# The first norm's gain and bias onto the residual: VectorE in sixteen pieces in place of GpSimd in eight

## The chip, the cores and the metric

One core of one Trainium2 chip runs the whole kernel. The metric is the device time of one execution in microseconds, as the median of several runs; the profile is of one further execution. Lower is better. The engines are called TensorE (PE in the rows, PEld for its weight loads), VectorE (DVE), ScalarE (ACT), GpSimd (POOL) and SyncE (SP, here only a queue that issues DMAs).

## What is computed

One decoder layer over 512 tokens of width 2048, all in float32. Cut to what matters here:

```python
mix = concat(sgu, hgrn2, mla) @ w_out
x   = layer_norm(ALPHA * x + mix, ln1_g, ln1_b)          # first norm
# mixture of experts: 32 experts, every token goes to 2 of them
for each expert e, on its own rows xb of x:
    h = silu(xb @ w_gate[e]) * (xb @ w_up[e])             # 2048 -> 512
    out[rows] += gate * (h @ w_down[e])                   # 512 -> 2048
x   = layer_norm(ALPHA * x + out, ln2_g, ln2_b)           # second norm
```

## The kernel before

**Where the first norm's vectors go.** The normalised rows without gain and bias are written to a DRAM tensor `x1d`, from which the experts gather their rows; gain and bias are put onto those by columns (`gcol`, in `rows`). The same normalised rows stay in SBUF as `z`, four tiles of 128 x 2048, one for each 128 tokens, since the second norm adds the experts' output to them. These copies must get gain and bias too, at any time before the last stage. Lines 1551 to 1559 do this in the expert loop: after expert 12's gate and up products the two vectors `ln1_g` and `ln1_b` are broadcast by DMA from the SP queue to two tiles of 128 x 2048 (`gb1`, 1 MB each), and in experts 13 to 20 GpSimd multiplies and adds one half (128 x 1024) of one `z` tile in each. After expert 21's products the same two slots are loaded with `ln2_g` and `ln2_b`, which the last stage reads (`lng2, lnb2`).

**One expert.** The loop over `e` calls `up(e)` (gate and up products, 16 weight chunks of 128 x 1024) and then `down(e - 1)` (8 chunks). A chunk is 512 KB. `Ring.pump` (lines 66 to 103) moves them: it issues the load from the SP queue as soon as a raw buffer is free (L81), and as soon as one of four pairs is free it splits the chunk into a high part (ScalarE copy, L96) and a low part (VectorE subtraction, L97), after which the raw buffer is free again. Four of the eight down chunks stay whole and are multiplied in full float32 (L1426). So an expert has 20 splits. A pair comes free when TensorE is done with the chunk (`ring.done`), so the splits run up to four pairs ahead of TensorE, and every instruction stands in its engine's queue in the order in which this program calls it.

**What else VectorE does in an expert.** `L1374` once at the start of `up(e)`; `L1364` half of the next expert's transposed rows; `L162` the low parts of those rows and of the hidden layer; `L1407` the product of gate and up for the next `down` (`turn_h`, called inside `down`, at its third chunk). ScalarE has the matching `L161`, and `L1430`, which takes each of the four 512-column outputs of `down` out of PSUM.

**What else GpSimd does.** In each expert a memset (L1328) and a gather (L1323) for expert e + 2 ahead of `up(e)`, and two scatter-adds (L1338) in `down(e - 1)`, which wait for L1430. The two multiplications and additions of lines 1558 and 1559 stand between them.

**Order around the change.** The lines stand after `up(e)` and after its pending `L162`, and ahead of `down(e - 1)`. On GpSimd the instruction in front of them is the gather, which is done early in the expert; on VectorE the one in front would be the last `L162` of `up(e)`, and the next ones the first two splits that `down(e - 1)` sets free.

Of the kernel before, what the change touches and what calls it, by code (L numbers as in the profile page):

```python
# [14 lines left out]
OP = mybir.AluOpType  # L15
# [8 lines left out]
DM = 2048  # L24
# [105 lines left out]
def build(tc, I, out):  # L130
    with ExitStack() as ctx:
        _build(tc, tc.nc, ctx, I, out)


def _build(tc, nc, ctx, I, out):
# [8 lines left out]
    def slot(tag, shape, dt=F32):  # L144
        cnt[0] += 1
        return bp.tile([P] + list(shape), dt, tag=tag, name=f"{tag}_{cnt[0]}")
# [5 lines left out]
    tt, ts, stt = nc.vector.tensor_tensor, nc.vector.tensor_scalar, nc.vector.scalar_tensor_tensor  # L152
# [74 lines left out]
    for k2 in range(8):  # L227
        t = slot(f"X{k2}", [2, 2, 512], F32R)
# [48 lines left out]
    def bcast(ap, n):  # L277
        return bass.AP(tensor=ap.tensor, offset=ap.offset, ap=[[0, P], [1, n]])
# [674 lines left out]
    z = [slot(t, [DM]) for t in ("B5", "B6", "B8", "B9")]  # L953
# [10 lines left out]
    gb1 = [slot("X7", [DM]), slot("B2", [DM])]  # L964
# [317 lines left out]
    def gates():  # L1282
        nc.gpsimd.tensor_tensor(gv, oh, wide(gate, [2 * NB, NE], 2), op=OP.mult)
        hl = tp[:, 0:512].rearrange("p (i a e) -> p i a e", a=2, e=NE)
        yield
        act(hl[:, :, 0], gv, AF.Copy)
        nc.gpsimd.tensor_tensor(hl[:, :, 1], gv, hl[:, :, 0].bitcast(F32), op=OP.subtract)
        yield
        o = aux()
        for i in range(2 * NB):  # L1290
            mm(o[:, 0:2 * NE], ohr[:, i // NB, i % NB], hl[:, i].rearrange("p a e -> p (a e)"),
               start=i == 0, stop=i == 2 * NB - 1)
        nc.vector.tensor_copy(gt, o[:, 0:NE])
        tt(gt, gt, o[:, NE:2 * NE], op=OP.add)
        yield
# [25 lines left out]
    def gather(e):  # L1321
        def move(n):
            nc.gpsimd.indirect_dma_start(out=xgs[e % 2][0:n, :], out_offset=None, in_=x1d[:],  # L1323
                                         in_offset=off(idx[0:n, EX[e]:EX[e] + 1]),
                                         bounds_check=T - 1, oob_is_err=False)
        if e:
            if e > 1:
                nc.gpsimd.memset(xgs[e % 2], 0.0)  # L1328
            sized(e, move)
        else:  # L1330

            move(32)
            with tc.If(nc.gpsimd.value_load(cnt_i[0:1, EX[0]:EX[0] + 1]) > 32):
                move(P)
# [20 lines left out]
    def rows(e, i, *by):  # L1355

        n = 4 // len(by)
        tmp = xgs[e % 2][:, i * 512:(i + 1) * 512]
        for h, ts in enumerate(by):
            o = turn(xgs[e % 2], i, range(h * n, h * n + n))  # L1360
            for j in range(h * n, h * n + n):
                g, b = [gcol[:, a, 4 * i + j:4 * i + j + 1] for a in range(2)]
                s = slice(j * P, (j + 1) * P)
                ts(tmp[:, s], o[:, s], g, b, op0=OP.mult, op1=OP.add)  # L1364
        def parts():
            d = [xT[i // 2][:, 4 * (i % 2):4 * (i % 2) + 4, :, a] for a in range(2)]
            split(d[0], d[1], tmp.rearrange("p (a t) -> p a t", t=P))
        return parts

    def up(e, hooks):  # L1370


        n = nc.tensor.value_load(cnt_i[0:1, EX[e]:EX[e] + 1])
        stt(folds[e % 2], pairs, few[:, EX[e]:EX[e] + 1], ident, op0=OP.mult, op1=OP.add)  # L1374
        for which in range(2):
            o = acc()
            for c in range(8):
                if (which, c) in hooks:
                    hooks[which, c]()
                if (which, c) == (1, 2):  # L1380
                    act(raws[0], fold(e, 0), AF.Silu)
                w = ring.get()
                ks = [(2 * c + j, [v[:, j * 512:(j + 1) * 512] for v in w]) for j in range(2)]
                with tc.If(n > HALF) as more:
                    for k, wk in ks:
                        mm3(o, [xT[k // 8][:, k % 8, :, a] for a in range(2)], wk, k == 0, k == KD - 1)
                with more.Else():
                    for k, wk in ks:
                        x = xT[k // 8][:, k % 8, 0:HALF].rearrange("p t a -> p (t a)")
                        mm(o, x, wk[0], start=k == 0, stop=False)  # L1390
                        mm(o, x, wk[1], start=False, stop=k == KD - 1)  # L1391
                if c == 7:
                    act(raws[which], o, AF.Copy)
                ring.done()
# [10 lines left out]
    def turn_h(e):  # L1405
        hi, lo = [v.rearrange("p a t -> p (a t)") for v in hTs[e % 2]]
        tt(hfs[e % 2], raws[0], fold(e, 1), op=OP.mult)  # L1407
        split(hi, lo, hfs[e % 2])
# [3 lines left out]
    def down(e):  # L1412
        if e in (0, NE - 1):
            yts.append(slot("M0" if e else "M1", [DM]))
        for n in range(4):
            o = acc()
            hT = hTs[e % 2]
            for c in range(2):
                if (n, c) == (1, 0) and e + 1 < NE:
                    turn_h(e + 1)  # L1420
                w = ring.get()
                for j in range(2):
                    k = 2 * c + j
                    cs = slice(j * 512, (j + 1) * 512)
                    if n in WHOLE:
                        mm(o, hfs[e % 2][:, k * P:(k + 1) * P], w[:, cs], start=k == 0, stop=k == 3)  # L1426
                    else:
                        mm3(o, (hT[0][:, k, :], hT[1][:, k, :]), (w[0][:, cs], w[1][:, cs]), k == 0, k == 3)
                if c:
                    act(yts[-1][:, n * 512:(n + 1) * 512], o, AF.Copy, scale=gt[:, EX[e]:EX[e] + 1])  # L1430
                ring.done()
            if e == NE - 1 and n == 1:
                scatter(e, 0)
        scatter(e, *([1] if e == NE - 1 else [0, 1]))
# [4 lines left out]
    def steps_of(e):  # L1439

        steps = {}
        for i in range(4):
            steps[(0, 2 * i + 1) if e > 1 else [(0, 5), (0, 6), (0, 7), (1, 1)][i]] = lambda i=i: later.append(rows(e, i, ts, gain_act))
            steps[1, 2 * i + 2] = lambda: later.pop(0)()
        return steps
# [74 lines left out]
    for e in range(NE):  # L1520
        if e and e + 2 < NE:
            gather(e + 2)
        hooks = steps_of(e + 1) if e + 1 < NE else {}
        if e == 0:
            rows(0, 1, gain_act)()
            hooks[0, 0] = lambda: later.append(rows(0, 2, ts, gain_act))

            def part3():
                later.pop()()
                later.append(rows(0, 3, ts, gain_act))  # L1530
            hooks[0, 2] = part3

            def last():
                later.pop()()
                gather(2)
            hooks[0, 4] = last
            gate_table = gates()
            for c in (0, 5, 7):
                hooks[1, c] = lambda: next(gate_table)
        if e == 1:  # L1540
            hooks[0, 2] = lambda: turn_h(0)
        up(e, hooks)
        while later:
            later.pop(0)()
        if e == 9:
            for entry in lent:
                entry[1] = True
        if e == NE - 3:
            for entry in ers:
                entry[1] = True  # L1550
        if e in (12, 21):
            gb1 = [slot("X7", [DM]), slot("B2", [DM])]
            for t, name in zip(gb1, ("ln1_g", "ln1_b") if e == 12 else ("ln2_g", "ln2_b")):
                nc.sync.dma_start(t, bcast(I[name], DM))
        if 13 <= e < 21:
            s = [slice(0, DM // 2), slice(DM // 2, DM)][(e - 13) % 2]
            b = (e - 13) // 2
            nc.gpsimd.tensor_tensor(z[b][:, s], z[b][:, s], gb1[0][:, s], op=OP.mult)  # L1558
            nc.gpsimd.tensor_tensor(z[b][:, s], z[b][:, s], gb1[1][:, s], op=OP.add)
        if e == 0:  # L1560
            x4 = slot("X4", [2, 1024])
            ring.add([x4[:, 0, :]])
            hfs += [x4[:, 1, i * DE:(i + 1) * DE] for i in range(2)]
            ring.add([misc[:, 1024:]])
            ring.pump()
        elif e < NE - 1:
            down(e - 1)
# [201 lines left out]
```

## Time and profile before

| | us |
|---|---|
| median of 3 runs | 1982.48 |
| lowest, highest | 1977.16, 1982.84 |
| the profiled execution | 1979.87 |
| its span, first to last instruction | 1978.1 |

The experts take some 1100 us of the span; in the experts VectorE is busy for some 86% and TensorE for some 96% of the time, and the granted TensorE clock is full except in short stretches. A row of the windows view gives, for a stretch in us from the span's start, the busy time of each engine with its count of instructions, the granted clock, the mean busy share of the DMA engines (its records overlap, so that it can pass 1) and GB/s. A row of the timeline gives start, duration, engine, line, operation, output and inputs and the count of merged instructions; in square brackets is how long the engine sat idle before it, and what ended that. Consecutive instructions of one engine may overlap by some 0.1 us, so that the distance of two starts is the better price of an instruction in a row of such.

### The profile page before, as it was taken

Reading aid. Unit: us, or ns where it says so; the run is one execution under the profiler, and the core shown is the slowest. Engines: PE = TensorE matmul, PEld = TensorE weight load, DVE = VectorE, ACT = ScalarE, POOL = GpSimd, SP = SyncE. Lnnn points to the kernel's source line nnn. Section 1 sums busy time; section 2 is a strip of 40 time slices with the busy share of each in tenths; the row PEclk is TensorE's granted clock in tenths of the full one; section 3 lists DMA queues with packets and bytes.
Section 4 is the critical chain, followed back from the end, with each engine's and each line's share of the span. In section 5 each row is a group of like instructions: output and inputs, shape, how many; then the busy total and the mean of one; then the engine's idle time right before and its main releaser. Section 6 shows DMA issues by size and latency. Waiting matters only on the chain.

```text
span 1978.1 us, 25265 instructions
## 1 busy us (share of the span) xinstructions
PE 1831.2 (93%) x8235; PEld 1382.6 (70%) x8236; DVE 1434.2 (73%) x1999; ACT 1265.4 (64%) x1763; POOL 325.1 (16%) x216
## 2 busy tenths in 40 slices
PE   9999999999999996899999999899999999999980
PEld 7888888887887895766666666666666666667640
DVE  5656432656554467879898988988898988888757
ACT  3633362745442225788787888777787888888753
POOL 1000000020000002121211213224323212121114
PEclk9999999999999996899999999899999999999995
DMA  7322213232173226899999999999899999999883
GB/s 250 100 77 75 86 64 107 86 123 90 43 262 107 93 89 222 290 369 389 388 379 393 356 372 393 359 368 343 311 356 347 386 394 392 396 377 381 284 288 142
DMA packets 139942, 510.72 MB, mean 258 GB/s; under 512 B 17664, under 2 KB 17712, under 8 KB 137200
## 3 DMA queue, kind: packets, MB, share of 16 engines
q1 hardware_dynamic: 130608, 476.64, 64.7%
q0 software_dynamic: 8576, 30.26, 5.9%
q8 instruction: 93, 1.52, 0.3%
q10 hardware_dynamic: 576, 1.57, 0.2%
q14 instruction: 89, 0.73, 0.1%
HBM read 488.53 MB, written 22.02 MB: 258 GB/s over the span
## 4 chain that ended last, share of the span: by engine, by line
issue 49%; PE 35%; POOL 8%; DVE 3%; DMA 2%; POOLq 1%; ACT 1%; SPq 0%; another core or an unknown queue 0%; ACTq 0%; DVEq 0%
PE acc L156 10%; PE acc L157 10%; PE acc L158 10%; POOL yd L1338 2%; POOL B L1328 2%; POOL M L1328 1%; POOL B L1558 1%; DMA yd<-M,idx 1%; PE aux L495 1%; POOLq L1309 1%; POOL M L1323 1%; DMA B<-x1d,idx 1%; PE acc L860 1%; POOL B L1323 0%; PE acc L861 0%
## 5 line engine op out<-in xcount | busy, mean ns | idle before, releaser
L97 DVE TENSOR_TENSOR whl<-X,whl 128x1024 fp32r<-128x1024 f32 x312 | 396.4, 1282 | 113.2 <-ACT whl L96 80.7
L97 DVE TENSOR_TENSOR whl<-wraw,whl 128x1024 fp32r<-128x1024 f32 (+1 forms) x222 | 280.7, 1267 | 232.5 <-ACT whl L96 212.9
L96 ACT ACTIVATE whl<-wraw 128x1024 fp32r<-128x1024 f32 (+1 forms) x222 | 234.2, 1058 | 226.9 <-PE acc L157 93.8
L96 ACT ACTIVATE whl<-X 128x1024 fp32r<-128x1024 f32 x312 | 328.9, 1066 | 64.9 <-PE acc L158 40.2
L1391 PE MATMUL acc<-whl,B 128*128 128x512 f32 x696 | 291.8, 419 | 36.1 <-DVE whl L97 36.1
L1390 PE MATMUL acc<-whl,B 128*128 128x512 f32 x696 | 298.2, 428 | 0.7 <-DVE B L162 0.7
L1338 POOL DMA_INDIRECT yd<-M,idx x64 | 90.0, 1406 | 855.5 <-ACT M L1430 855.5
L1391 PEld LDWEIGHTS acc<-whl,B 128*128 128x128 f32 x696 | 134.2, 193 | 106.7 <-DVE whl L97 78.0
L158 PE MATMUL acc<-whl,B 128*128 128x512 f32 (+1 forms) x480 | 181.4, 378 | 0.0
L157 PE MATMUL acc<-whl,B 128*128 128x512 f32 (+1 forms) x424 | 166.0, 392 | 15.0 <-DVE whl L97 14.9
L156 PE MATMUL acc<-whl,B 128*128 128x512 f32 (+1 forms) x424 | 179.2, 423 | 0.1
L1390 PEld LDWEIGHTS acc<-whl,B 128*128 128x128 f32 x696 | 134.4, 193 | 31.1 <-issue 7.8
L156 PE MATMUL acc<-X,whl 128*128 128x512 f32 x384 | 151.0, 393 | 0.3 <-ACT X L161 0.3
L157 PE MATMUL acc<-X,whl 128*128 128x512 f32 x384 | 149.7, 390 | 0.6 <-DVE X L162 0.6
L158 PE MATMUL acc<-X,whl 128*128 128x512 f32 x384 | 149.6, 390 | 0.0
L1426 PE MATMUL acc<-X,X 128*128 128x512 f32 x308 | 141.2, 592 | 0.0
L97 DVE TENSOR_TENSOR X<-X,X 128x1024 fp32r<-128x1024 f32 x105 | 127.9, 1218 | 16.8 <-ACT X L96 12.6
L1430 ACT ACTIVATE M<-acc,X 128x512 f32<-128x512 f32 x128 | 87.4, 683 | 68.5 <-PE acc L1426 57.7
L96 ACT ACTIVATE X<-X 128x1024 fp32r<-128x1024 f32 x105 | 111.9, 1066 | 24.5 <-PE acc L158 15.4
L157 PEld LDWEIGHTS acc<-whl,B 128*128 128x128 f32 x424 | 80.5, 190 | 48.5 <-DVE whl L97 27.7
L1391 PE MATMUL acc<-X,B 128*128 128x512 f32 x232 | 100.1, 432 | 8.4 <-DVE X L97 8.4
L158 PEld LDWEIGHTS acc<-whl,B 128*128 128x128 f32 x480 | 91.0, 189 | 15.7
(461 smaller groups left out, 3699.3 us busy)
## 6 DMA issues: line engine op xcount, KB each, us to landing
X<-w_down SPq DMA_DIRECT2D x169, 512.0 KB
X<-w_gate SPq DMA_DIRECT2D x160, 512.0 KB
X<-w_up SPq DMA_DIRECT2D x160, 512.0 KB
wraw<-w_gate SPq DMA_DIRECT2D x69, 512.0 KB
wraw<-w_up SPq DMA_DIRECT2D x69, 512.0 KB
wraw<-w_in SPq DMA_DIRECT2D x64, 512.0 KB
wraw<-w_down SPq DMA_DIRECT2D x64, 512.0 KB
B<-w_up SPq DMA_DIRECT2D x27, 512.0 KB
```

The source lines that it names most:

```text
L96: nc.scalar.activation(h[:, s], r[:, s], AF.Copy)
L97: nc.vector.tensor_tensor(l[:, s], r[:, s], h[:, s].bitcast(F32), op=OP.subtract)
L156: mm(o, a[0], b[0], start=start, stop=False)
L157: mm(o, a[0], b[1], start=False, stop=False)
L158: mm(o, a[1], b[0], start=False, stop=stop)
L495: mm(ov[r, j], fl(D)[:, c * P:c * P + r.stop], Dv[:, c, :, 1, :], start=True, stop=True)
L1328: nc.gpsimd.memset(xgs[e % 2], 0.0)
L1338: nc.gpsimd.indirect_dma_start(out=yd[i][:], out_offset=off(index), in_=y[:, H[i]], in_offset=None, bounds_check=T - 1, oob_is_err=False, ...
L1390: mm(o, x, wk[0], start=k == 0, stop=False)
L1391: mm(o, x, wk[1], start=False, stop=k == KD - 1)
L1426: mm(o, hfs[e % 2][:, k * P:(k + 1) * P], w[:, cs], start=k == 0, stop=k == 3)
L1430: act(yts[-1][:, n * 512:(n + 1) * 512], o, AF.Copy, scale=gt[:, EX[e]:EX[e] + 1])
```

## The change

The eight pairs of GpSimd instructions on 128 x 1024 become sixteen pairs of VectorE instructions on 128 x 512, one pair in each of experts 13 to 28. `tt` is VectorE's `tensor_tensor`. The load of the second norm's vectors moves from expert 21 to expert 29, since the slots are read up to expert 28.

```diff
-        if e in (12, 21):
+        if e in (12, 29):
             gb1 = [slot("X7", [DM]), slot("B2", [DM])]
             for t, name in zip(gb1, ("ln1_g", "ln1_b") if e == 12 else ("ln2_g", "ln2_b")):
                 nc.sync.dma_start(t, bcast(I[name], DM))
-        if 13 <= e < 21:
-            s = [slice(0, DM // 2), slice(DM // 2, DM)][(e - 13) % 2]
-            b = (e - 13) // 2
-            nc.gpsimd.tensor_tensor(z[b][:, s], z[b][:, s], gb1[0][:, s], op=OP.mult)
-            nc.gpsimd.tensor_tensor(z[b][:, s], z[b][:, s], gb1[1][:, s], op=OP.add)
+        if 13 <= e < 29:
+
+            b, s = (e - 13) // 4, slice((e - 13) % 4 * 512, ((e - 13) % 4 + 1) * 512)
+            for t, op in zip(gb1, (OP.mult, OP.add)):
+                tt(z[b][:, s], z[b][:, s], t[:, s], op=op)
```

## Rows read from the trace of the kernel before

**Rows 1.** The page's head: span, then busy time of each engine, share, instructions.
```profile
span 1978.1 us, 25265 instructions
PE 1831.2 (93%) x8235; PEld 1382.6 (70%) x8236; DVE 1434.2 (73%) x1999; ACT 1265.4 (64%) x1763; POOL 325.1 (16%) x216
```

**Rows 2.** Windows, one expert each: 13, 14, 17, 20, 22, then 29.
```profile
1221.80:1259.50 37.70, 33.62 (x137) 23.86 (x136) 33.14 (x36) 29.25 (x40) 11.84 (x6) 0.95 1.02 396
1259.50:1298.40 38.90, 34.76 (x138) 24.11 (x137) 34.33 (x37) 29.19 (x40) 12.88 (x6) 0.91 0.95 332
...
1375.10:1414.50 39.40, 38.79 (x169) 29.33 (x168) 33.37 (x36) 30.27 (x40) 12.61 (x6) 1.00 0.93 337
...
1491.30:1530.20 38.90, 34.75 (x139) 24.09 (x137) 34.33 (x37) 29.14 (x40) 12.84 (x6) 0.91 0.95 346
...
1564.20:1598.30 34.10, 32.62 (x139) 22.42 (x137) 29.54 (x37) 28.72 (x40) 6.10 (x4) 1.00 1.03 394
...
1802.60:1840.90 38.30, 38.30 (x169) 29.52 (x168) 30.55 (x36) 30.22 (x40) 5.54 (x4) 1.00 0.98 355
```

**Rows 3.** Timeline of GpSimd early in expert 13.
```profile
1228.35 2.49 POOL L1558 TENSOR_TENSOR B<-B,X 128x1024 f32<-128x1024 f32 x1
1230.92 3.23 POOL L1559 TENSOR_TENSOR B<-B,B 128x1024 f32<-128x1024 f32 x1
```

**Rows 4.** Lines 1558 and 1559: durations in ns (least, median, most), first and last start.
```profile
L1558 POOL TENSOR_TENSOR B<-B,X x8: 2373/2432/2750, 1228.3 to 1499.1; 128x1024 f32<-128x1024 f32 x8
L1559 POOL TENSOR_TENSOR B<-B,B x8: 3232/3239/3261, 1230.9 to 1501.5; 128x1024 f32<-128x1024 f32 x8
```

**Rows 5.** Timeline of VectorE in the same stretch.
```profile
1227.38 1.22 DVE L97 TENSOR_TENSOR whl<-B,whl 128x1024 fp32r<-128x1024 f32 x1
...
1229.15 6.09 DVE L97 TENSOR_TENSOR whl<-X,whl 128x1024 fp32r<-128x1024 f32 x2
```

**Rows 6.** Timeline of TensorE in the same stretch.
```profile
1231.98 0.50 PE L1391 MATMUL acc<-whl,B 128*128 128x512 f32 x1 [0.86 <-DVE whl L97]
1235.29 0.50 PE L1391 MATMUL acc<-whl,B 128*128 128x512 f32 x1 [2.12 <-DVE whl L97]
```

**Rows 7.** Timeline of VectorE over expert 22, undisturbed.
```profile
1564.21 0.34 DVE L1374 SCALAR_TENSOR_TENSOR R<-R,identr 128x128 f32<-128x128 f32 x1
1566.91 1.23 DVE L97 TENSOR_TENSOR whl<-B,whl 128x1024 fp32r<-128x1024 f32 x1 [2.35 <-issue]
...
1589.44 0.69 DVE L162 TENSOR_TENSOR B<-B,B 128x512 fp32r<-128x512 f32 x1
1590.04 1.22 DVE L97 TENSOR_TENSOR whl<-X,whl 128x1024 fp32r<-128x1024 f32 x1
...
1593.69 0.69 DVE L162 TENSOR_TENSOR B<-X,B 128x512 fp32r<-128x512 f32 x1 [0.70 <-ACT B L161]
1595.24 1.23 DVE L97 TENSOR_TENSOR whl<-X,whl 128x1024 fp32r<-128x1024 f32 x1 [0.86 <-ACT whl L96]
1597.12 1.22 DVE L97 TENSOR_TENSOR whl<-X,whl 128x1024 fp32r<-128x1024 f32 x1 [0.66 <-ACT whl L96]
1598.27 0.34 DVE L1374 SCALAR_TENSOR_TENSOR R<-R,identr 128x128 f32<-128x128 f32 x1
```

**Rows 8.** TensorE's weight loads, waits from 1530 to 1802: total us, times, longest.
```profile
PEld acc L1391 <- DVE whl L97: 16.4, 32, 1.0
```

**Rows 9.** Timeline of ScalarE at the end of expert 22.
```profile
1593.02 0.63 ACT L161 ACTIVATE B<-X 128x512 fp32r<-128x512 f32 x1 [3.00 <-DVE X L1407]
...
1598.89 0.69 ACT L1430 ACTIVATE M<-acc,X 128x512 f32<-128x512 f32 x1 [1.80 <-PE acc L1426]
```

**Rows 10.** Timeline of VectorE at 428: a dependent pair of the wanted shape, the next.
```profile
428.74 0.68 DVE L743 TENSOR_TENSOR M<-aux,B 128x512 f32<-128x512 f32 x1
429.46 0.69 DVE L744 TENSOR_TENSOR M<-M,B 128x512 f32<-128x512 f32 x1
430.07 0.96 DVE L673 TENSOR_TENSOR X<-X,R 128x256 f32<-128x256 f32 x1
```

**Rows 11.** Line 1554, the vectors' loads: first and last start.
```profile
L1554 SPq DMA_DIRECT2D X<-ln_g x2: 423/444/464, 1213.4 to 1555.9; - x2
```

**Rows 12.** Windows: experts 21 to 28 together, and a stretch across expert 29's end.
```profile
1530.20:1802.60 272.40, 260.92 (x1089) 178.99 (x1088) 235.90 (x281) 229.86 (x320) 55.37 (x32) 1.00 1.03 388
1832.00:1856.00 24.00, 23.63 (x100) 16.27 (x99) 18.50 (x24) 19.04 (x28) 2.78 (x2) 1.00 0.75 237
```

**Rows 13.** ScalarE's only wait for a weight load from 1530 to 1802.
```profile
ACT whl L96 <- DMA X<-w_up: 0.3, 1, 0.3
```

## The prediction

> **What bounds the kernel now.** The page's head comes first: TensorE is busy for 93% of the span, VectorE for 73%, GpSimd for 16% [rows 1]. Such averages say little here, so the second view cuts the expert stage into windows, one for each expert, from one L1374 to the next. An ordinary expert takes 34.06 us (1564.21 to 1598.27, [rows 7]); the eight from 21 to 28 take 272.4 us together, 34.05 each, at full clock [rows 12]. The eight with GpSimd's two instructions, 13 to 20, run from 1221.8 to 1530.2, which is 308.4 us, with a granted clock of 0.91 to 0.95 in the ordinary ones among them [rows 2]; the three windows left out there look like the first two. So the loss is in those eight, and the third view, the timelines of one of them, shows how it comes about. GpSimd's multiplication runs from 1228.35 for 2.49 us and its addition from 1230.92 for 3.23 us [rows 3]; meanwhile two splits L97 on VectorE take 6.09 us, where one takes 1.22 us just before [rows 5]. TensorE then stands for 0.86 and 2.12 us, waiting for exactly these splits [rows 6], and its clock falls to the lower level for a while afterwards, which is what the 0.95 and 0.91 of [rows 2] show.
>
> In an ordinary expert VectorE has two phases. From 1566.91 to about 1593 it runs without a gap, and TensorE's weight loads wait for its splits, four times an expert (32 waits, 16.4 us in eight experts, [rows 8]): here VectorE sets the pace. At the expert's end it is idle for 0.70, 0.86, 0.66 and, in the next expert's first microseconds, 2.35 us [rows 7], 4.57 us in all, since the pairs are full and TensorE works on whole chunks: here TensorE sets it. What is slowed in the first phase is lost; what is added in the second can hide.
>
> The Trainium skill (SBUF — State Buffer, section "Who interferes with whom") says that a VectorE instruction with two SBUF inputs and a GpSimd instruction that reads SBUF exclude each other for a whole instruction, by issue order. The trace agrees: the second split ends at 1235.24, 1.09 us after GpSimd's addition. By that rule alone the eight pairs (2.432 + 3.239 us, [rows 4]) could hold VectorE for 45.4 us; the sum below goes by the windows instead, which count only what TensorE lost.
>
> **The change part by part.**
>
> *GpSimd's sixteen instructions go.* Seven of the eight experts should return to 34.06 us. Expert 17 has more rows (169 matmuls instead of 137 to 139, 39.4 us, [rows 2]); expert 29, with the same count and no GpSimd work, takes 38.3 us with TensorE busy all the time [rows 2]. So the stretch becomes 7 x 34.06 + 38.3 = 276.7 us, a gain of 308.4 - 276.7 = 31.7 us. If expert 17 fell to 34.06 as well, the gain would be 35.9; that is the other end. Gathers and scatters on GpSimd have nothing in front of them any more; they wait for L1430 anyway.
>
> *VectorE gets a pair of 128 x 512 in each of sixteen experts.* The trace has such a pair, the second in place on the first's result: starts at 428.74, 429.46, and the next instruction at 430.07 [rows 10], so 1.33 us for a pair and 21.3 us for sixteen. The pair comes between the last L162 of the gate and up products (1589.44) and the first split that down sets free (1590.04, [rows 7]). That is the end of the first phase: the splits delayed are the next expert's first ones, which TensorE wants only after 1598. I follow the 1.33 us. The two splits, then L1407, come 1.33 us later; ScalarE's L161, which already waits 3.00 us for L1407 [rows 9], waits 4.33, and behind it stand the evacuation of the second output and the copies for the next two splits. ScalarE's cover is the 1.80 us before the L1430 at 1598.89, which waits for TensorE [rows 9]; VectorE's is the 2.35 us ahead of the fifth gate split, which waits for a pair that TensorE frees [rows 7]. Both exceed 1.33 us, so the fifth split, from which VectorE sets the pace again, starts when it did. Cost 0, with 21.3 us as the upper end if none of it hides; I take 0 because both covers are shown in an ordinary expert, and a gain is excluded, as work is only added. The first scatter-add follows its evacuation 1.33 us later, with nobody waiting. Raw buffers of the delayed splits come free 1.33 us later, and behind them on the SP queue stand the next loads; loads arrive early enough that ScalarE waited for one only once, 0.3 us, in eight experts [rows 13].
>
> *The new waits.* The first pair waits for the loads of gain and bias, issued at 1213.4 [rows 11], over 30 us ahead of its place in expert 13. The second norm's load waits on the SP queue for expert 28's pair, done an expert earlier; behind it stand the weight loads, which so wait for nothing.
>
> *The load of 2 MB moves from expert 21 to 29.* At 394 GB/s [rows 2] it takes 5.3 us of DMA time. In expert 21 it was hidden: experts 21 to 28 are all ordinary. In expert 29 it will be issued near 1832, where the DMA engines run at 0.75 of their time against 1.03 in the stage before, 24 us long [rows 12]: 24 x 0.28 = 6.7 us are free, more than 5.3. Bounds 0 and 5.3; I take 0.5, as the last experts have fewer raw buffers.
>
> *The load in expert 12 loses its cover.* Until now the slow experts 13 to 20 followed it and let the DMAs catch up. The nearest row is expert 21's load, which no slow expert followed, at no cost. Bounds 0 and 5.3; I take 0.5.
>
> Sum: 1978.1 - 31.7 + 0 + 0.5 + 0.5 = 1947.4 us of span, and 1.8 us lie around the span (1979.87 - 1978.1), so 1949.2. The profiled execution is 2.6 us under the median of the runs and within their spread (1977.16 to 1982.84); I put the median of the new kernel at 1950.
>
> **The rivals.**
>
> *A, the pair doesn't hide.* If ScalarE's later chain makes the next expert's splits late after all, each pair costs its 1.33 us: 1949.2 + 21.3 = 1970.5. For it: VectorE is close to its limit and ScalarE is tied to L1407. Against: both covers above. It decides when the delay passes 1.80 us.
>
> *B, the DMAs become the bound.* At 1.03 [rows 12] the DMA engines have little left, and sixteen ordinary experts now follow one another. Price: both 2 MB loads in full, 10.6 us, so 1959.8. Against: experts 21 to 28 held 34.05 us at 388 GB/s right after such a load. The Trainium skill (SBUF — State Buffer, section "A bandwidth-pool intuition that's wrong (but worth ruling out)") gives some 358 GB/s from HBM to a core; held to that, an expert of 34.05 us at 388 GB/s would take an estimated 36.9 us, and some 20 us of the gain would be gone. The trace shows 388 over eight experts, so that doesn't hold here.
>
> *C, slower: the pair starts a stall that brings the clock down.* In expert 13 waits of 0.86 and 2.12 us [rows 6] were followed by the lower clock. If the pair's 1.33 us reaches TensorE as one wait and the clock then falls for a few microseconds, as in expert 13 (5% of 37.7 us is 1.9 us lost, [rows 2]), each expert pays about 1.33 + 1.9 = 3.2 us, sixteen pay 52, and the time is 1949.2 + 52 = 2001. It decides at 31.7 / 16 = 2.0 us for each pair. Against: the pair stands in the phase in which TensorE has four split chunks ahead, and the waits of up to 1.0 us in ordinary experts [rows 8] go with a clock of 1.00.
>
> *D, the change doesn't remove the cause.* If the slow splits had another cause in experts 13 to 20, the time would stay near 1980. Against: the splits are long just while rows 3's instructions run.
>
> **How the numbers follow.** Chances: forecast 0.76, A 0.09, B 0.08, C 0.05, D 0.02. The forecast with its bounds spans 1943 (expert 17 at 34.06, and the lower runs) to 1956; the range goes up to 1965 to take in B with the runs' spread, and leaves out A, C and D, 16 in 100. A difference of 0.3%, about 6 us, is what a measurement of this kernel can tell from none. Faster by more: forecast, B and nearly all of A, 0.92. Within: D and a rest of A, 0.03. Slower: C, 0.05.
>
> **What would show it.** Right: experts 13 to 16 at 34.0 to 34.2 us, clock 1.00, no L97 above 1.3 us, expert 17 near 38.3; the new pair of 1.33 us after the last L162, ScalarE's wait for L1407 at about 4.3 us, and VectorE's idle 2.35 us shrunk to about 1. Experts 21 to 28, so far undisturbed, are the test of the pair alone: they should stay at 34.05 us in spite of it. Wrong: 35.4 us there (A), ScalarE waiting for weight loads in 13 to 20 or after 1855 (B), a clock under 1.00 (C), or L97 at 3 us as before (D).

## The result, and the profile after

The changed kernel takes 1945.94 us (median of 4 runs, 1945.13 to 1946.49), the kernel before, measured beside it, 1980.67 us (4 runs). The ratio is 0.983 with a 95% interval of 0.9817 to 0.9843: 34.7 us less. The profiled execution took 1946.49 us. The head of its page:

```profile
span 1944.7 us, 25279 instructions
PE 1818.7 (94%) x8235; PEld 1370.1 (70%) x8236; DVE 1422.1 (73%) x2031; ACT 1260.5 (65%) x1763; POOL 277.1 (14%) x200
```

Against [rows 1] GpSimd has 16 instructions less and VectorE 32 more, and yet VectorE is busy for 12.1 us less: its own 32 are cheaper than what GpSimd's 16 had cost it. The windows, one expert each (13, 14, 17), then experts 21 to 28 together; columns as in [rows 2]:

```profile
1220.40:1255.40 35.00, 33.59 (x141) 22.99 (x140) 30.80 (x38) 28.96 (x41) 7.26 (x4) 1.00 1.03 397
1255.40:1289.50 34.10, 32.66 (x138) 22.47 (x137) 30.83 (x39) 28.64 (x41) 7.25 (x4) 1.00 1.03 392
...
1358.40:1395.00 36.60, 36.60 (x164) 28.26 (x162) 31.77 (x39) 29.34 (x39) 6.45 (x4) 1.00 1.01 386
...
1498.10:1770.60 272.50, 261.02 (x1090) 179.10 (x1089) 246.32 (x298) 228.77 (x321) 55.31 (x32) 1.00 1.02 384
```

The granted clock is 1.00 throughout and the ordinary expert is back at 34.1 us. One thing has to be known to read such windows: an expert is cut off at VectorE's L1374, and the new pair itself moves this mark by 0.94 us against TensorE's work (35.00 - 34.06), once, in expert 13, and back in expert 29. In the experts around 17 the mark moves again: experts 16 to 18 take 34.94 + 36.53 + 34.99 us, which is two ordinary experts and 38.34 us. Experts 13 to 20 run from 1220.4 to 1498.1, 277.7 us, or 276.8 without the moved mark, instead of 308.4 [rows 2].

VectorE at the end of expert 22, the answer to [rows 7]:

```profile
1522.38 0.69 DVE L162 TENSOR_TENSOR B<-M,B 128x512 fp32r<-128x512 f32 x1
1522.99 0.68 DVE L1559 TENSOR_TENSOR B<-B,X 128x512 f32<-128x512 f32 x1
1523.71 0.69 DVE L1559 TENSOR_TENSOR B<-B,B 128x512 f32<-128x512 f32 x1
1524.32 1.22 DVE L97 TENSOR_TENSOR whl<-X,whl 128x1024 fp32r<-128x1024 f32 x1
...
1529.49 1.22 DVE L97 TENSOR_TENSOR whl<-X,whl 128x1024 fp32r<-128x1024 f32 x1 [0.83 <-ACT whl L96]
1531.01 1.23 DVE L97 TENSOR_TENSOR whl<-X,whl 128x1024 fp32r<-128x1024 f32 x1 [0.30 <-ACT whl L96]
...
1533.90 1.23 DVE L97 TENSOR_TENSOR whl<-B,whl 128x1024 fp32r<-128x1024 f32 x1 [1.40 <-issue]
```

The pair takes 1524.32 - 1522.99 = 1.33 us, and the idle times behind it have shrunk from 0.66 to 0.30 and from 2.35 to 1.40. ScalarE's waits from 1498.1 to 1770.6 (total us, times, longest), against [rows 9, 13]:

```profile
ACT B L161 <- DVE X L1407: 34.5, 8, 4.3
ACT M L1430 <- PE acc L1426: 7.8, 9, 0.9
...
ACT whl L96 <- DMA X<-w_up: 0.3, 1, 0.3
```

It waits 4.3 us instead of 3.0 for L1407: ScalarE, too, is 1.33 us late there. It makes that up in its later waits for TensorE, of which the one before the evacuation that closes the expert shrinks from 1.8 to 0.9 us. VectorE makes it up in its own: 0.03 of the 0.86 us, 0.36 of the 0.66 and 0.95 of the 2.35, 1.34 us in all.

**Where the 33.4 us of span went.** Experts 13 to 20: 31.6. Experts 21 to 28: nothing (272.49 against 272.45 us). The rest, about 1.8, lies ahead of expert 13 (1.4, before any changed instruction) and behind expert 28 (0.4). In some executions the work ahead of the first expert takes longer (its L1374 starts at 783 to 784 us in the profiles of e3, e7 and e8, at 776 to 778 in all others), so the experiments are compared by stretches of experts as well as by their times.

### The profile page after: what moved, and what is told of

Its sections match the earlier page's. It is cut to its first block, busy times and chain, and to the rows that moved or that the text cites. A ratio compares the mean times of both kernels' runs of the same rounds, so it can differ in the third digit from the quotient of the medians.

```text
span 1944.7 us, 25279 instructions
## 1 busy us (share of the span) xinstructions
PE 1818.7 (94%) x8235; PEld 1370.1 (70%) x8236; DVE 1422.1 (73%) x2031; ACT 1260.5 (65%) x1763; POOL 277.1 (14%) x200
## 4 chain that ended last, share of the span: by engine, by line
issue 50%; PE 36%; POOL 6%; DVE 4%; DMA 2%; POOLq 1%; ACT 0%; another core or an unknown queue 0%; SPq 0%; ACTq 0%; DVEq 0%
PE acc L156 10%; PE acc L157 10%; PE acc L158 10%; POOL yd L1338 2%; POOL B L1328 2%; POOL M L1328 1%; DMA yd<-M,idx 1%; POOLq L1309 1%; PE aux L495 1%; PE acc L860 1%; DMA B<-x1d,idx 1%; DVE B L1617 0%; PE acc L861 0%; POOLq L1315 0%; PE aux L831 0%
## 5 line engine op out<-in xcount | busy, mean ns | idle before, releaser
L97 DVE TENSOR_TENSOR whl<-X,whl 128x1024 fp32r<-128x1024 f32 x312 | 377.4, 1221 | 100.0 <-ACT whl L96 68.5
L97 DVE TENSOR_TENSOR whl<-wraw,whl 128x1024 fp32r<-128x1024 f32 (+1 forms) x222 | 269.6, 1217 | 227.6 <-ACT whl L96 210.1
L1391 PE MATMUL acc<-whl,B 128*128 128x512 f32 x696 | 288.2, 414 | 15.6 <-DVE whl L97 15.6
L1390 PE MATMUL acc<-whl,B 128*128 128x512 f32 x696 | 295.0, 424 | 1.4 <-ACT whl L96 0.7
L1391 PEld LDWEIGHTS acc<-whl,B 128*128 128x128 f32 x696 | 132.0, 190 | 86.8 <-DVE whl L97 59.5
L1390 PEld LDWEIGHTS acc<-whl,B 128*128 128x128 f32 x696 | 132.0, 190 | 31.8 <-issue 4.3
L97 DVE TENSOR_TENSOR X<-X,X 128x1024 fp32r<-128x1024 f32 x105 | 128.0, 1219 | 17.5 <-ACT X L96 13.2
L157 PEld LDWEIGHTS acc<-whl,B 128*128 128x128 f32 x424 | 80.5, 190 | 47.7 <-DVE whl L97 27.0
L158 PEld LDWEIGHTS acc<-whl,B 128*128 128x128 f32 x480 | 91.0, 190 | 15.7
```

The lines of the kernel that those rows point to most:

```text
L97: nc.vector.tensor_tensor(l[:, s], r[:, s], h[:, s].bitcast(F32), op=OP.subtract)
L157: mm(o, a[0], b[1], start=False, stop=False)
L158: mm(o, a[1], b[0], start=False, stop=stop)
```

## The experiments

The forecast's theory was that GpSimd's instructions hold up VectorE's splits, for which TensorE waits, and that VectorE's own pair hides at the expert's end. The main rivals: the pair shows (A), the DMAs set the pace (B), the pair stalls TensorE and lowers its clock (C).

### The pair taken away, and the pair put elsewhere

e1 leaves out the pair:

```diff
-            for t, op in zip(gb1, (OP.mult, OP.add)):
-                tt(z[b][:, s], z[b][:, s], t[:, s], op=op)
+            pass
```

> The changed kernel without the sixteen VectorE pairs (the first norm's gain and bias are left out of the residual), loads unchanged. Theory (the pair of 1.33 us lies in VectorE's idle time at an expert's end): the same time as the changed kernel, 1944 to 1947 us, experts at 34.05, VectorE's idle time before the fifth gate split back from 1.40 to about 2.35 us and ScalarE's wait for L1407 back from 4.25 to about 3.0. Rival A (part of the pair shows): faster by up to 21 us, 1925.

Measured: 1946.86 us, ratio to the kernel before 0.9848 (0.9825 to 0.987); the changed kernel, run again as e9, took 1946.61 (0.9843). Experts 21 to 28 take 272.49 us with the pair and without it. ScalarE's waits in them are back:

```profile
ACT B L161 <- DVE X L1407: 23.9, 8, 3.0
ACT M L1430 <- PE acc L1426: 14.4, 8, 1.8
```

Sixteen pairs, 21.3 us of VectorE's time, cost nothing that shows. A falls for the place in which the pair stands.

e2 calls the same pair inside the gate product:

```diff
+        if 13 <= e < 29:
+            def pair(b=(e - 13) // 4, s=slice((e - 13) % 4 * 512, ((e - 13) % 4 + 1) * 512)):
+                for t, op in zip(gb1, (OP.mult, OP.add)):
+                    tt(z[b][:, s], z[b][:, s], t[:, s], op=op)
+            hooks[0, 6] = pair
         up(e, hooks)
```

> The same sixteen pairs, called at the seventh chunk of the gate product, where VectorE runs without a gap and TensorE waits for its splits. Theory of the two phases: each pair costs its 1.33 us, 16 x 1.33 = 21 us, so 1967 us, experts 13 to 28 at 35.4. Rival (VectorE's idle time is a common reserve, its place doesn't matter): 1946, experts at 34.05.

Measured: 1965.47 us. VectorE around the pair, experts 21 to 28 in one window, and a wait of TensorE right behind the pair:

```profile
1587.37 0.68 DVE L1545 TENSOR_TENSOR B<-B,X 128x512 f32<-128x512 f32 x1
1588.09 0.69 DVE L1545 TENSOR_TENSOR B<-B,B 128x512 f32<-128x512 f32 x1
1588.70 1.22 DVE L97 TENSOR_TENSOR whl<-X,whl 128x1024 fp32r<-128x1024 f32 x1
```

```profile
1505.20:1788.30 283.10, 263.98 (x1091) 179.01 (x1089) 246.23 (x298) 233.91 (x320) 50.78 (x32) 1.00 1.01 370
```

```profile
1589.97 0.50 PE L1391 MATMUL acc<-whl,B 128*128 128x512 f32 x1 [0.37 <-DVE whl L97]
```

283.1 / 8 = 35.39 us an expert: each pair costs its 1.33 us. Only expert 17, in which TensorE is busy throughout, pays nothing (38.29 us). So the pair's place in VectorE's order, not VectorE's busy share, decides. The clock stays at 1.00 although TensorE waits for the pair. But the delay reaches it in pieces. Its waits for such splits in experts 21 to 28 (total us, times, longest), which were 8 of 0.6 us at most without the early pair:

```profile
PE acc L1391 <- DVE whl L97: 12.0, 24, 0.6
```

The single wait of 1.33 us that C assumed didn't occur and wasn't tried.

### How much fits

e3 and e4 apply gain and bias two and three times at the place of the change:

```diff
-            for t, op in zip(gb1, (OP.mult, OP.add)):
+            for t, op in zip(gb1 * 2, (OP.mult, OP.add) * 2):      # e4: * 3
```

> Gain and bias are applied twice, at the place of the change: 4 dependent instructions, 3 x 0.72 + 0.61 = 2.8 us in each of sixteen experts. Theory (the cover is what is left in ScalarE's and VectorE's waits, some 0.9 and 1.4 us after the first pair): the second pair of 1.44 us passes ScalarE's cover by about 0.5 us, of which the following wait for TensorE takes 0.3, so 0 to 0.5 us an expert, 0 to 9 us in all, 1946 to 1955; I expect 1950. Rival (each instruction shows): 1969.

> Gain and bias are applied three times: 6 instructions, 4.2 us in each of sixteen experts, against a cover of about 2.5 us in all. Theory: 1.7 us an expert show, 27 us in all, 1973, experts 13 to 28 at 35.8. Rival (each instruction shows): 1946 + 46 = 1992. Rival C (once a wait reaches TensorE its clock falls as well): over 2000, with a granted clock below 1.00 in those experts.

Measured: e3 1949.59 us (runs from 1945.82 to 1953.23), e4 1967.81 us. The windows of experts 21 to 28, first of e3, then of e4:

```profile
1506.00:1779.10 273.10, 261.68 (x1090) 179.24 (x1089) 257.37 (x314) 226.74 (x321) 54.48 (x33) 1.00 1.02 384
```

```profile
1509.40:1794.10 284.70, 265.84 (x1089) 179.33 (x1088) 268.42 (x330) 227.04 (x321) 54.42 (x33) 1.00 1.00 368
```

An expert takes 34.14 us with 2.77 us of added work and 35.59 with 4.21, so 0.08 and 1.53 us more than the ordinary 34.06. Both give the same cover: 2.77 - 0.08 = 2.69 and 4.21 - 1.53 = 2.68 us. The timeline of VectorE in e4 shows what it consists of:

```profile
1649.08 1.22 DVE L97 TENSOR_TENSOR whl<-wraw,whl 128x1024 fp32r<-128x1024 f32 x1 [0.83 <-ACT whl L96]
1650.61 1.23 DVE L97 TENSOR_TENSOR whl<-X,whl 128x1024 fp32r<-128x1024 f32 x1 [0.30 <-ACT whl L96]
...
1652.13 1.23 DVE L97 TENSOR_TENSOR whl<-wraw,whl 128x1024 fp32r<-128x1024 f32 x1
```

The 2.35 us ahead of the fifth split [rows 7] are used up, and of the 0.66 us 0.30 are left: 2.35 + 0.36 = 2.71 us. The other waits, 0.70 and 0.83, belong to the chain from L1407 over ScalarE and move along with it; they are no cover. ScalarE runs out at the same point. Its copy for the fifth split, in the kernel before and then in e4 with the L161 at the chain's start:

```profile
1599.87 1.06 ACT L96 ACTIVATE whl<-wraw 128x1024 fp32r<-128x1024 f32 x1 [0.28 <-PE acc L1391]
```

```profile
1646.90 0.63 ACT L161 ACTIVATE B<-X 128x512 fp32r<-128x512 f32 x1 [7.19 <-DVE X L1407]
...
1651.04 1.06 ACT L96 ACTIVATE whl<-wraw 128x1024 fp32r<-128x1024 f32 x1
```

From the start of L161 to the end of that copy ScalarE takes 5.20 us, without a gap, where it took 7.91 before (1593.02 [rows 9] to 1600.93): 2.71 us less. So both engines have some 2.7 us to give, and these runs don't tell which of the two sets the limit.

### The engine, the size and the load, each by itself

e5 is the changed kernel with its sixteen small pieces on GpSimd:

```diff
-                tt(z[b][:, s], z[b][:, s], t[:, s], op=op)
+                nc.gpsimd.tensor_tensor(z[b][:, s], z[b][:, s], t[:, s], op=op)
```

> The changed kernel's sixteen pieces of 128 x 512, but on GpSimd: only the engine differs from the change. Theory (GpSimd's two-input instructions hold up VectorE's splits for as long as they run, about 1.3 + 1.7 us a pair): an expert loses about half of what it lost with the larger pieces, 1.9 instead of 3.7 to 4.8 us, in twice as many experts: 1946 + 16 x 1.9 = 1976. If the shorter waits no longer bring TensorE's clock down, about 1.5 us each, 1970. Rival (the smaller pieces make the gain, not the engine): 1946.

Measured: 1982.57 us, ratio 1.0015 (0.9996 to 1.0034) to the kernel before: all of the gain is gone. GpSimd and VectorE in one expert of e5, and TensorE behind them:

```profile
1556.23 1.29 POOL L1559 TENSOR_TENSOR B<-B,X 128x512 f32<-128x512 f32 x1
1557.60 2.16 POOL L1559 TENSOR_TENSOR B<-B,B 128x512 f32<-128x512 f32 x1
```

```profile
1555.85 2.77 DVE L97 TENSOR_TENSOR whl<-X,whl 128x1024 fp32r<-128x1024 f32 x1
1558.54 2.30 DVE L97 TENSOR_TENSOR whl<-wraw,whl 128x1024 fp32r<-128x1024 f32 x1
```

```profile
1558.67 0.50 PE L1391 MATMUL acc<-whl,B 128*128 128x512 f32 x1 [0.86 <-DVE whl L97]
1560.90 0.50 PE L1391 MATMUL acc<-whl,B 128*128 128x512 f32 x1 [1.04 <-DVE whl L97]
```

From 1555.85 to 1560.84 the two splits take 4.99 us instead of 2.35 for two in a row, 2.6 more, and experts 21 to 28 take 293.2 us (36.65 each, 2.6 more). The direction was expected, the size, 1.9 us an expert, was not. The loss comes in two sizes. In expert 13 of the kernel before VectorE has this instruction at the start of GpSimd's multiplication (1228.35, [rows 3]); its data come from PSUM, and it isn't held up:

```profile
1228.51 0.73 DVE L1364 TENSOR_SCALAR M<-aux,X 128x128 f32<-128x128 f32 x2
```

Where an L1364 stands so, an expert loses 3.7 to 3.8 us there (13, 15, 19) and 1.6 in e5 (15, 16, 20); where a split is already up, 4.8 to 4.9 us there (14, 16, 18, 20) and 2.6 in the other twelve of e5 (expert 17 aside). I had halved the smaller of the two, and most experts of e5 pay the larger.

e6 is the kernel before with only the load moved (`if e in (12, 29)` for `if e in (12, 21)`):

> The kernel before with only the second norm's load moved from expert 21 to expert 29, GpSimd's work unchanged. Theory (the load is hidden in either place): the same as the kernel before within 2 us. Rival (the load costs its 5.3 us among the last experts' loads): 5 us slower. Rival (the move is part of the gain): 2 to 3 us faster.

Measured: 1979.86 us beside 1979.85, ratio 1.0006 (0.9989 to 1.0023). Its experts 13 to 20, then 21 to 28:

```profile
1220.30:1530.60 310.30, 279.06 (x1123) 197.86 (x1121) 272.33 (x282) 234.33 (x320) 101.55 (x48) 0.93 0.97 347
1530.60:1803.00 272.40, 260.87 (x1089) 179.02 (x1088) 235.86 (x281) 229.88 (x320) 53.07 (x32) 1.00 1.02 382
```

From the end of expert 28 to the end of the span, with the moved load in it, both profiles take 175.5 us (1978.1 - 1802.6 before). The load is hidden in either place, and its move has no part in the gain.

e7 is the kernel before with VectorE for GpSimd and nothing else:

```diff
-            nc.gpsimd.tensor_tensor(z[b][:, s], z[b][:, s], gb1[0][:, s], op=OP.mult)
-            nc.gpsimd.tensor_tensor(z[b][:, s], z[b][:, s], gb1[1][:, s], op=OP.add)
+            for t, op in zip(gb1, (OP.mult, OP.add)):
+                tt(z[b][:, s], z[b][:, s], t[:, s], op=op)
```

> VectorE in experts 13 to 20 with the kernel before's pieces of 128 x 1024, the load left in expert 21: only the engine differs from the kernel before. A pair takes about 1.26 + 1.14 = 2.4 us, near the end of a cover of 2.5 us. Theory: as fast as the change or up to 3 us slower, 1946 to 1949. Rival (the smaller pieces matter, the larger ones stall TensorE): 8 x 1 us or more, over 1954.

Measured: 1948.33 us, ratio 0.9835 (0.9808 to 0.9863), against 0.983 and 0.9843 of the changed kernel. Its experts 14, 19 and 20 take 34.05 to 34.07 us. The engine makes the gain; sixteen small pieces are not measurably better than eight large ones, whose some 2.4 us a pair still lie within the cover of 2.7.

e8 replaces each of GpSimd's two instructions by a copy with one input:

```diff
-            nc.gpsimd.tensor_tensor(z[b][:, s], z[b][:, s], gb1[0][:, s], op=OP.mult)
-            nc.gpsimd.tensor_tensor(z[b][:, s], z[b][:, s], gb1[1][:, s], op=OP.add)
+            for _ in range(2):
+                nc.gpsimd.tensor_copy(z[b][:, s], gb1[0][:, s])
```

> The kernel before, GpSimd's two instructions each replaced by a copy of 128 x 1024 with one SBUF input (the residual is overwritten by the gain, so gain and bias are left out). Theory (whatever GpSimd reads in SBUF holds up VectorE's two-input splits): each expert still loses about the copies' own time, some 2 us or more, so 1955 to 1975, with splits L97 of over 2 us. Rival (only GpSimd's two-input instructions hold VectorE up): 1946, L97 at 1.22 us throughout.

Measured: 1957.87 us, ratio 0.9884 (0.9858 to 0.991). GpSimd, then VectorE, in expert 14; the memset in front runs beside VectorE's splits of 1.22 us:

```profile
1263.72 2.34 POOL L1328 MEMSET M<- 128x2048 f32 x1
...
1268.89 3.04 POOL L1559 COPY B<-X 128x1024 f32<-128x1024 f32 x2
```

```profile
1265.64 1.22 DVE L97 TENSOR_TENSOR X<-X,X 128x1024 fp32r<-128x1024 f32 x1
...
1268.55 4.46 DVE L97 TENSOR_TENSOR whl<-X,whl 128x1024 fp32r<-128x1024 f32 x2
```

Two splits beside 3.04 us of copies take 4.46 us instead of 2.35, and an expert 36.1 to 36.2 us, 2.1 more (expert 13, where L1364 comes first, 35.1). So a second input of GpSimd isn't needed to hold the splits up, while a memset, which reads nothing, holds nothing up. The Trainium skill (SBUF — State Buffer, section "Who interferes with whom") puts the line there too: a VectorE instruction with two SBUF inputs contends with a GpSimd instruction that reads SBUF, not with one that only writes it. The traces agree: 4.46 us for two splits beside the copies, 1.22 us for one beside the memset.

### VectorE's work moved out of the first phase

If VectorE's place decides, its other work can be moved too. The low parts of the next expert's rows (L162) are made at three places inside the up product and one behind it. e10 moves one more behind it, to the place of the pair, e11 two; e9 is the changed kernel beside them.

```diff
         for i in range(4):
             ...
-            steps[1, 2 * i + 2] = lambda: later.pop(0)()
+            if i in (0, 1, 3):                                     # e11: (0, 3)
+                steps[1, 2 * i + 2] = lambda: later.pop(0)()
```

> The changed kernel once more, beside the two that follow on the same chip: 1945 to 1953 us, experts at 34.05 us.

> The changed kernel, with one of the three low parts L162 (and its copy L161 on ScalarE) that VectorE makes within the gate and up products called after them instead, at the place of the pair. It moves 0.60 us of VectorE's work in each of about 30 experts out of the phase in which VectorE sets the pace into the one in which it is idle. With the pair that makes 1.33 + 0.60 = 1.9 us of a cover of 2.7 us. Theory of the two phases: an expert takes 34.05 - 0.6 = 33.45 us, 18 us in all, 1928. Rival (the DMAs, at 1.03 of their time, allow no faster expert): 33.8 us or more, 1938 to 1946, with ScalarE waiting for weight loads. Rival (no such phases): 1946.

> The same with two of the three low parts moved: 1.2 us of VectorE's work an expert, and 1.33 + 1.2 = 2.5 us of a cover of 2.7 us. Theory of the two phases alone: 32.85 us an expert, 1910. With the DMAs as the next bound, which I expect by then: about as fast as with one moved, 1925 to 1940, and ScalarE waits for weight loads in every expert.

Measured: e9 1946.61, e10 1947.74, e11 1936.89 us; e11's ratio to the kernel before is 0.9796 (0.9779 to 0.9812), the fastest here. e10 was a miss: no gain at all. Its VectorE in expert 8, then TensorE's last wait for a split in that expert:

```profile
1071.33 1.21 DVE L97 TENSOR_TENSOR whl<-X,whl 128x1024 fp32r<-128x1024 f32 x1
1072.47 1.21 DVE L97 TENSOR_TENSOR X<-B,X 128x1024 fp32r<-128x1024 f32 x1
1073.60 2.35 DVE L97 TENSOR_TENSOR whl<-X,whl 128x1024 fp32r<-128x1024 f32 x2
1075.88 1.28 DVE L162 TENSOR_TENSOR B<-B,B 128x512 fp32r<-128x512 f32 x2
```

```profile
1072.60 0.50 PE L157 MATMUL acc<-whl,B 128*128 128x512 f32 x1 [0.54 <-DVE whl L97]
```

The last split for which TensorE waits ends near 1072.5. The moved L162 had stood behind the split of 1072.47, which is already past that point, so it had cost nothing where it was. e11 also moves the one that stood ahead of the split awaited at 1072.60, and there the expert shortens by its 0.60 us. Windows of e11: experts 2 to 12, 13 to 20, 21 to 28, then the same of e9:

```profile
846.00:1213.00 367.00, 357.14 (x1495) 245.59 (x1493) 324.06 (x385) 315.94 (x440) 71.52 (x44) 1.00 1.03 386
1213.00:1492.50 279.50, 270.00 (x1127) 186.94 (x1126) 248.45 (x298) 232.53 (x321) 51.84 (x32) 1.00 1.02 383
1492.50:1762.50 270.00, 262.62 (x1097) 180.09 (x1096) 246.82 (x298) 230.97 (x321) 52.97 (x33) 1.00 1.03 389
```

```profile
846.30:1220.30 374.00, 358.30 (x1495) 245.79 (x1494) 324.02 (x384) 316.05 (x440) 69.25 (x44) 1.00 1.02 380
1220.30:1498.20 277.90, 267.87 (x1125) 186.74 (x1124) 247.72 (x298) 231.00 (x321) 51.94 (x32) 1.00 1.02 385
1498.20:1770.50 272.30, 260.78 (x1089) 178.94 (x1088) 246.16 (x297) 228.53 (x321) 53.06 (x32) 1.00 1.02 384
```

In experts 3 to 11 an expert takes 33.45 us, and the first stretch is 7.0 us shorter. Experts 19 to 26 run at 33.45 us again:

```profile
1425.60:1693.20 267.60, 260.60 (x1090) 179.05 (x1089) 246.51 (x298) 230.64 (x320) 51.89 (x32) 1.00 1.03 390
```

Between them, behind the load of expert 12, the gain is lost. Experts 13 to 18 take 212.6 us; five at 33.45, one at 38.3 and an estimated 1.3 for the moved mark (there the wait of 2.15 us in VectorE's expert 8 shrinks to 0.78 in expert 21) would be 206.9. ScalarE's waits of e11 from 1213 to 1492.5 show where it goes:

```profile
ACT whl L96 <- DMA X<-w_down: 10.8, 6, 2.8
```

The weight loads, for which ScalarE waited only once in eight experts of the kernel before [rows 13], come late there. The 5.7 us are close to the 5.3 that rival B set for one load of 2 MB: with shorter experts it no longer hides. I had expected such waits in every expert, but from expert 2 to 12 none is listed, and experts 19 to 26 keep 33.45 us at 390 GB/s. Experts 27 and 28 take 34.81 and 34.49 us, again with late weight loads, and why is open. e11 wasn't run with the load elsewhere, so the load as the cause is read from the place and the waits only.

## Why the prediction was right, point by point

**GpSimd's instructions: right in cause and size.** Forecast for experts 13 to 20 was 276.7 us; it became 276.8, with the clock at 1.00, expert 17 at 38.3 (by the sum above; 38.29 directly in e2) and L97 at 1.22 us on average. e5, e7 and e8 show that the engine, and that it reads SBUF, is the cause. That the price had to be read from the windows rather than from GpSimd's busy time is confirmed by expert 17: GpSimd was just as busy there, and it gave back 1.1 us only. The loss of an expert was just what its two splits lost. In expert 13 they took 6.09 us [rows 5] instead of 2.35, 3.74 more, and the expert 37.78 (L1374 at 1221.77 and 1259.55) instead of 34.06, 3.72 more; in expert 14 they lost 4.77 and the expert, with 38.83 us, 4.77:

```profile
1266.93 7.12 DVE L97 TENSOR_TENSOR whl<-X,whl 128x1024 fp32r<-128x1024 f32 x2
```

So the 45.4 us that I worked out from GpSimd's durations were too much, as the addition's seem to hold a wait of its own (last section). A slip: [rows 2] leave out four windows between the first and the last of experts 13 to 20, not three; they too took 37.8 to 39.0 us at a clock of 0.91 to 0.95.

**The pair on VectorE: cost 0, right.** 1.33 us as priced; experts 21 to 28 took 34.06 us each with it; e1 without it is no faster. VectorE's wait of 2.35 us shrank to 1.40, not to about 1, since the 0.66 us in front gave 0.36.

**The cover: mis-sized.** I put the point from which rival A decides at 1.80 us, ScalarE's one wait. e3 and e4 measure 2.69. On VectorE 0.36 of the 0.66 us count beside the 2.35. ScalarE has two further waits for TensorE in the same chain, shown as 0.25 and 0.28 us, beside its 1.80; by the distances of starts the three are worth 2.7. And the end of the first phase, which I read off VectorE's gapless stretch as 1593 in expert 22, is earlier: it is the split for which TensorE waits last, as e10 and e11 show. Neither changed the forecast, because the pair stood behind both points and its 1.33 us are under 1.80 as well.

**The two loads: 0.5 us each forecast, nothing found.** e6 shows none for the moved one (1.0006, an interval of some 3 us either way, and 175.5 us behind expert 28 with it and without it); for the load of expert 12 the sum of experts 13 to 20 leaves no room for one.

**The remainder.** Forecast were 1949.2 us for an execution like the profiled one and 1950 for the median, measured 1946.49 and 1945.94. Of the 2.7 us between the profiled ones, 1.0 are the loads and 1.8 lie ahead of expert 13 and behind expert 28, outside the change. The 0.8 us added for the median weren't needed either.

**The rivals.** A: real in the first phase (e2) and beyond 2.69 us (e4), not here. B: not at 34.06 us an expert; at 33.45 (e11) the load of 2 MB shows, while the weight loads alone still keep up. The estimate from the Trainium skill's table (SBUF — State Buffer, section "A bandwidth-pool intuition that's wrong (but worth ruling out)": 358 GB/s, from it 36.9 us) doesn't hold, as experts 21 to 28 ran at 384 GB/s. The Trainium skill (HBM Reference, section "Specifications (TRN2)") also says that a core that streams alone gets well more than that share. The trace agrees, with 384 GB/s; with the neighbouring core at work it wasn't tried. C: the clock stayed at 1.00 in e2 and e4, where TensorE did pay for the delay, though in waits of at most 0.6 us in e2 and 1.0 in e4. Its term of 1.9 us for the clock has no room in the trace of the kernel before: there the experts lost what the splits lost, and no more. D fell with e7.

## What to carry to other kernels

Work on an engine that is nearly idle is not free: GpSimd's, when it reads SBUF, held up VectorE's splits, which have two SBUF inputs. Price it by the stretch in which the other engine sets the pace, not by its own busy share. An engine that is busy for 90% can still take some more work at no cost if that stands behind the last result that the bound engine waits for, and how much fits is found by putting in two and three times as much. Before moving work out of such a stretch, look whether it stands ahead of that last awaited result; behind it there is nothing to win.

## What the runs showed of the hardware that was not expected

GpSimd's two instructions are unequal: the addition takes 3.24 us where the multiplication of the same shape takes 2.43 [rows 4], and at half the size 2.16 and 1.29. The difference fits a wait of the addition for VectorE. In e5's rows above the first split ends at 1558.62, 1.10 us after the multiplication, and the addition ends 1.14 us after that; the second split ends 1.08 us after the addition. A split alone takes 1.14 us from start to start, so the four seem to run one at a time, and the addition's own time would be some 1.14 us, not 2.16. That is read from the rows and wasn't tested apart. Which of two goes first doesn't follow the recorded starts: the first split is recorded 0.38 us ahead of the multiplication and was held all the same, so that the order of issue, by which the prediction lets them exclude each other, isn't shown here.

TensorE's clock fell after the longer of its waits in the kernel before (0.91 to 0.95 in an expert), and hardly in e5, where the single waits are about 1 us (0.98 in experts 21 to 28):

```profile
1511.80:1805.00 293.20, 267.33 (x1089) 182.65 (x1088) 256.77 (x281) 234.53 (x320) 85.27 (x48) 0.98 0.99 357
```
